# One-column products for the first group's sums of squares, and a fixed order for row 0 of the opening loop

## The chip, the cores and the metric

The kernel runs on one core of a Trainium2 chip. The metric is the device time of one execution in microseconds (us). A core has five engines with a queue of instructions each: TensorE (PE, its weight loads are listed as PEld), VectorE (DVE), ScalarE (ACT), GpSimd (POOL) and SyncE (SP), which here only issues transfers. All wait for one another through semaphores.

## The reference

One layer of a hybrid mixer over 2048 tokens of 1024 columns, with 256 context tokens beside them. What matters here is its beginning:

```python
def rms_norm(x):
    return x * lax.rsqrt(jnp.mean(x * x, axis=-1, keepdims=True) + EPS)

shift, scale, gate = jnp.split(jax.nn.silu(c) @ w_ada[l] + b_ada[l], 3, axis=-1)
h = rms_norm(x) * (1.0 + scale[:, None, :]) + shift[:, None, :]
rq, rk, rv, rg, aq, ak, av, ag = project(h, w_in[l])      # h @ w_in, 13 chunks of 256 columns
```

Behind it stand retention, windowed attention, the output projection, the gated residual and a last norm.

## The kernel before

Tokens are taken in four groups of 512, group 3 first. A group is held transposed: 8 tiles of 128 model columns by 512 tokens, the "rows" k = 0 to 7 of the opening loop. Each operand of a projection is split into a high part, rounded to fp32r, and a low part, the remainder; a projection is three products for each row: high by high, high by low, low by high.

Opening, lines 905 to 952. The row `c` is loaded, spread to all partitions by a product with ones (L205) and put through SiLU on ACT (L206). Group 3 is loaded in four transfers of two rows (`x3`). For each of the four ACT squares one row (L926), DVE the other (L927) and adds them (L928), and PE adds over partitions with a product of 512 columns (L929), so that every partition holds the sums of all 512 tokens. Four DVE instructions then take the diagonal of each 128x128 block (L934), DVE forms the mean (L181), POOL raises it to the power -0.5 (L184), DVE lays the roots out on four diagonals (L189), and PE spreads these to all partitions by products with ones (`spread`, L196). Twelve dummy products on a tile of ones (`warm`, L915) stand in three places.

The opening loop (L972 to 1000) runs over k. `ada` loads two tiles of 128x1024 of the conditioning matrix (`wss`), and DVE multiplies each by the SiLU row and sums it up (`weigh`, L215); with the bias added (L226) this is the shift and scale of 128 columns. At each even k four transfers bring two rows of four chunks of `w_in`; ACT rounds the high parts (L111), DVE and, for chunk `rg1`, POOL take the low parts (L970). `modulate` scales the row (DVE, L231), ACT adds the shift and rounds (`h3h`, L232), and DVE takes the remainder (`h3l`, L233). PE then runs 24 products for the row (L993) into eight banks. Behind the loop come the roots of the next group (L997, from sums of squares that ACT takes of rows of `x`, L176), the weights of chunk `aq0` (L111 and L329), the gates, whose ACT instructions (L591) free banks, and the products of `aq0` (L341).

The program is written in one sequence; a scheduler orders the instructions of each engine by a model of costs and due times, except where `tc.keep_in_program_order` pins an instruction behind all that was written before it on its engine, or `tc.issue_after` (in `behind`) puts those of a block behind a named one on its engine. These order the issue only; each engine runs its queue strictly in order.

Of the kernel before, what the change touches and what calls it, by code (L numbers as in the profile page):

```python
# [16 lines left out]
P = 128  # L17
# [22 lines left out]
def tile_hymba(  # L40
# [111 lines left out]
    class Stats:  # L152
# [24 lines left out]

        def roots(self, on_dve=False):
            r = rsm.tile([P, 2, 4], F32, tag="rs", name=f"r_{self.name}")
            if on_dve:  # L180
                PE["mean"] = dve.tensor_scalar(r[:, 1, : self.nt], self.ss, 1.0 / D, EPS, op0=ALU.mult, op1=ALU.add)  # L181
            else:
                act.activation(r[:, 1, : self.nt], self.ss, AF.Identity, bias=eps1, scale=1.0 / D)
            pool.tensor_tensor(r[:, 0, : self.nt], r[:, 1, : self.nt], half4[:, : self.nt], op=ALU.pow)  # L184
            self.dg = tmp(f"dg_{self.name}")[:, : self.n]
            for t in range(self.nt):
                dst, rt = self.dg[:, t * P : (t + 1) * P], r[:, 0, t : t + 1]
                if on_dve:
                    PE["diag"] = dve.tensor_scalar(dst, ident, rt, None, op0=ALU.mult)  # L189
                else:  # L190
                    act.activation(dst, ident, AF.Copy, scale=rt)

# [7 lines left out]
    def silu_row(t, i):  # L200
        nc.sync.dma_start(t[0:1], crow[i : i + 1])
        for n in range(2):
            s = slice(n * GT, (n + 1) * GT)
            ps = ptp.tile([P, GT], F32, tag="tp", name=f"pc{i}{n}")
            pe.matmul(ps, ones[0:1], t[0:1, s], start=True, stop=True)  # L205
            act.activation(t[:, s], ps, AF.Silu)  # L206
        return t

    def weigh(w, row, a, idle=False):

        if idle:
            pool.tensor_tensor(w, w, row, op=ALU.mult)
            act.activation(w, w, AF.Copy, accum_out=a)
        else:
            dve.scalar_tensor_tensor(w, w, 1.0, row, op0=ALU.mult, op1=ALU.mult, accum_out=a)  # L215

# [3 lines left out]
    def ada(pl, tag, row, kc, which, after=(None, None)):  # L220
        for j in range(2):
            w = pl.tile([P, D], F32, tag=tag, name=f"wss{which}_{kc}_{j}")
            nc.sync.dma_start(w, wss[kc][:, j, :])
            with behind(after[j]):
                weigh(w, row, acc2[:, kc, which, j : j + 1], which and j)
        dve.tensor_tensor(mod[:, kc, which], acc2[:, kc, which], nbada[:, kc:16:8], op=ALU.add)  # L226

    def modulate(x, r, which, ht, k):

        shk, sck = mod[:, k, which, 0:1], mod[:, k, which, 1:2]  # L230
        PE["scaled"] = dve.scalar_tensor_tensor(x, x, sck, r, op0=ALU.mult, op1=ALU.mult)  # L231
        act.activation(ht[0][:, k, :], x, AF.Identity, bias=shk)  # L232
        return dve.scalar_tensor_tensor(ht[1][:, k, :], x, shk, ht[0][:, k, :], op0=ALU.add, op1=ALU.subtract)  # L233
# [682 lines left out]

    row0 = silu_row(st0.tile([P, D], F32, tag="row", name="row0", bufs=1), 0)
# [5 lines left out]
    pss = ptp.tile([P, GT], F32, tag="tp", name="ss_x3")  # L923
# [28 lines left out]

    def start_weights(q):

        for pair in range(2):
            raw = ld.tile([P, 2, 2, 256], F32, tag="ld", name=f"wr_s{pair}_{q}")
            for i in range(2):
                n = CH[2 * pair + i]
                nc.sync.dma_start(raw[:, i], win[CHUNKS.index(n)][:, 2 * q : 2 * q + 2, :])
            for i in range(2):  # L960
                n = CH[2 * pair + i]
                rounded(startw[n][:, 0, 2 * q : 2 * q + 2, :], raw[:, i], "act")
                raws[n] = raw[:, i]

    raws = {}
# [6 lines left out]
    for k in range(NK):  # L972
        ada(st0, "ada", row0, k, 0, (PE["scaled"],) * 2 if k else (PE["mean"], PE["diag"]))
        if k % 2 == 0:
            start_weights(k // 2)
            with behind(None if k else PE["diag"]):
                start_low(k // 2, CH if k else CH[:1])
        modulate(x3[:, k], r3 if k else ps3, 0, H[3], k)
        if k == 0:
            with behind(PE["scaled"]):  # L980
                start_low(0, CH[1:])
            r3 = rp.tile([P, GT], F32, tag="rope", name="r3")
            act.activation(r3, ps3, AF.Copy)
        if k == NK - 2:
# [421 lines left out]
```

## Time and profile before

| | us |
|---|---|
| three timed runs | 1178.88, 1181.79, 1182.34 (median 1181.79) |
| the profiled execution | 1177.99 |
| its span, first to last instruction | 1175.4 |
| PE busy | 1133.2 (96%) |
| DVE busy | 798.2 (68%) |
| ACT busy | 465.7 (40%) |
| POOL busy | 404.5 (34%) |

The profile is of one execution, and its own time is 2.6 us above its span. All moments below are microseconds from the start of the span. Matmuls are pipelined, so a record's length is longer than the step from one to the next. A granted clock of 1.00 is the higher of TensorE's two levels (2.4 GHz), 0.50 the lower (1.2 GHz).

### The profile page before, as it was taken

What the parts mean: (1) busy time and instruction counts of PE and PEld (TensorE: products, weight loads), DVE (VectorE), ACT (ScalarE), POOL (GpSimd) and SP (SyncE); (2) the same over time, 40 slices, a digit from 0 to 9 for tenths busy, and PEclk for the clock granted to TensorE, in tenths of its full rate; (3) what the DMA queues carried; (4) which work ended last, traced back from release to release, by engine and by line L of the source; (5) the groups of instructions that cost most, each with busy time, mean ns of one, the idle gap of its engine ahead of it and who ended that gap; (6) DMA issues with size and microseconds to landing.
All of it is one profiled execution on the core that took longest, in us unless ns stands there. A gap on an engine that the chain in (4) does not pass through costs nothing.

```text
span 1175.4 us, 18111 instructions
## 1 busy us (share of the span) xinstructions
PE 1133.2 (96%) x6290; PEld 973.1 (83%) x6290; DVE 798.2 (68%) x1883; ACT 465.7 (40%) x1025; POOL 404.5 (34%) x517
## 2 busy tenths in 40 slices
PE   7999978999999999999999988999999999999997
PEld 3887857999988889998888877888888888888885
DVE  6974876544783645657666447777777777777774
ACT  3344423432342002331001336555555555555562
POOL 1102654100221200002224335555555555555542
PEclk9998989999999999999999999999999999999999
DMA  8948678542564542533356385444444444444310
GB/s 305 324 152 259 235 228 308 177 132 86 176 215 157 162 125 77 175 119 117 97 162 201 83 210 187 131 130 131 130 130 131 131 130 131 130 130 131 95 37 36
DMA packets 139537, 182.24 MB, mean 155 GB/s; under 512 B 11315, under 2 KB 103091, under 8 KB 139318
## 3 DMA queue, kind: packets, MB, share of 16 engines
q1 hardware_dynamic: 126630, 174.54, 47.3%
q10 hardware_dynamic: 12816, 6.56, 1.8%
q8 instruction: 49, 0.80, 0.3%
q14 instruction: 42, 0.34, 0.1%
HBM read 130.19 MB, written 50.86 MB: 154 GB/s over the span
## 4 chain that ended last, share of the span: by engine, by line
PE 69%; DVE 19%; POOL 3%; ACT 3%; DMA 3%; issue 2%; SPq 1%; DVEq 0%; POOLq 0%; ACTq 0%
PE pz L1205 10%; PE rv L354 8%; PE rk L341 7%; PE aq L341 6%; PE ag L341 6%; PE o L1168 4%; PE rg L341 4%; PE rq L341 4%; PE pt L1155 3%; DVE p L749 3%; DVE phl L1158 3%; PE S L743 3%; PE u L470 2%; PE ak L341 2%; PE S L747 2%
## 5 line engine op out<-in xcount | busy, mean ns | idle before, releaser
L1157 ACT ACTIVATE phl<-pt 128x512 fp32r<-128x512 f32 x156 | 92.7, 595 | 98.8 <-PE pt L1155 96.0
L765 POOL TENSOR_SCALAR p<-p,m 128x640 f32<-128x640 f32 (+1 forms) x128 | 104.1, 814 | 69.9 <-DVE m L764 68.5
L1158 DVE TENSOR_TENSOR phl<-pt,phl 128x512 fp32r<-128x512 f32 x156 | 106.8, 686 | 29.9 <-ACT phl L1157 29.2
L756 ACT ACTIVATE p<-p,m 128x641 f32<-128x641 f32 (+1 forms) x128 | 104.5, 816 | 47.3 <-DVE m L753 47.0
L749 DVE CUSTOM_DVE_ANT_0 p<-S,msk 128x640 f32<-128x640 f32 (+1 forms) x128 | 102.5, 801 | 23.4 <-PE S L747 22.0
L1205 PE MATMUL pz<-wg1h,ma 128*128 128x512 f32 x256 | 106.0, 419 | 0.1
L1205 PE MATMUL pz<-wg0h,mr 128*128 128x512 f32 x256 | 104.0, 409 | 0.6 <-POOL mr L1194 0.4
L1155 PE MATMUL pt<-ident,p 128*128 128x128 f32 x624 | 94.0, 273 | 0.0
L743 PE MATMUL S<-kwin,aq 128*128 128x384 f32 (+1 forms) x256 | 79.2, 332 | 4.2 <-DVE m L749 2.8
L1155 PEld LDWEIGHTS pt<-ident,p 128*128 128x128 f32 x624 | 75.8, 141 | 8.7 <-issue 0.4
L446 ACT ACTIVATE vw<-v,wdec 128x128 fp32r<-128x128 f32 x128 | 43.5, 393 | 80.1 <-DVE v L459 80.1
L747 PE MATMUL S<-kctx,aq 128*128 128x256 f32 x256 | 71.1, 280 | 0.0
L1168 PE MATMUL o<-phl,vwin 128*128 128x512 f32 x184 | 63.1, 422 | 0.8 <-DVE phl L1158 0.6
L743 PEld LDWEIGHTS S<-kwin,aq 128*128 128x128 f32 x256 | 48.0, 188 | 10.7 <-DVE m L749 3.4
L1205 PEld LDWEIGHTS pz<-wg0h,mr 128*128 128x128 f32 x256 | 48.1, 188 | 9.3 <-POOL mr L1194 0.8
L1205 PEld LDWEIGHTS pz<-wg1h,ma 128*128 128x128 f32 x256 | 48.1, 188 | 7.9 <-POOL ma L1183 0.5
L747 PEld LDWEIGHTS S<-kctx,aq 128*128 128x128 f32 x256 | 48.2, 188 | 5.3
L1168 PE MATMUL o<-phl,vctx 128*128 128x512 f32 x128 | 44.7, 414 | 6.8 <-DVE phl L1158 6.7
L1205 PE MATMUL pz<-wg0l,mr 128*128 128x512 f32 x128 | 50.5, 395 | 0.0
L1205 PE MATMUL pz<-wg1l,ma 128*128 128x512 f32 x128 | 50.3, 393 | 0.0
L448 DVE SCALAR_TENSOR_TENSOR vw<-v,wdec,vw 128x128 fp32r<-128x128 f32 x128 | 39.9, 358 | 6.2 <-ACT vw L446 6.2
L780 POOL TENSOR_TENSOR qd<-qkv,decq 128x512 f32<-128x512 f32 x30 | 42.3, 1428 | 1.1
(430 smaller groups left out, 3067.7 us busy)
## 6 DMA issues: line engine op xcount, KB each, us to landing
wss<-in_wss SPq DMA_DIRECT2D x32, 512.0 KB, 6.3
qkv<-d_qkv SPq DMA_DIRECT2D x15, 768.0 KB, 6.2
aq<-d_aq SPq DMA_DIRECT2D x64, 128.0 KB, 3.9
xb<-in_xn SPq DMA_DIRECT2D x16, 512.0 KB, 4.2
out<-xb SPq DMA_DIRECT2D x31, 256.0 KB, 2.3
st<-d_st SPq DMA_DIRECT2D x15, 512.0 KB, 3.8
x<-in_xt SPq DMA_DIRECT2D x12, 512.0 KB, 5.3
xr_x<-in_xn SPq DMA_DIRECT2D x12, 512.0 KB, 3.8
```

Source lines behind the costliest of these rows:

```text
L341: pe.matmul(ps, w[:, a, k, c0 : c0 + P], ht[b][:, k, :], start=(k == 0 and i == 0), stop=(k == NK - 1 and i == 2),)
L354: pe.matmul(ps, ht[a][:, k, t * P : (t + 1) * P], w[:, b, k, :], start=(k == 0 and i == 0), stop=(k == NK - 1 and i == 2),)
L743: i = pe.matmul(psc[:, o:512].rearrange("p (s t) -> p s t", t=P), AQ[b][:, h, :], C2["kwin"][:, kv, hl, ksel], start=(hl == 0), stop=(hl = ...
L747: pe.matmul(psc[:, 512:768], AQ[b][:, h, :], C2["kctx"][:, kv, hl], start=(hl == 0), stop=(hl == 1))
L749: dve.tensor_tensor_reduce(out=pb[:, j, 0:n], in0=psc[:, o : o + n], in1=mk, op0=ALU.add, op1=ALU.max, scale=1.0, scalar=-3e38, accum_out= ...
L756: act.activation(pb[:, j, 0 : n + 1], pb[:, j, 0 : n + 1], AF.Exp, bias=m4[:, 1, j : j + 1], scale=0.125, accum_out=m4[:, 2, j : j + 1],)
L765: pool.tensor_scalar(pb[:, j, 0:n], pb[:, j, 0:n], m4[:, 2, j : j + 1], 0.0, op0=ALU.mult, op1=ALU.add)
L1155: pe.transpose(ppt[:, j], pb[:, j, kt * P : (kt + 1) * P], ident)
L1157: PE["phl"] = act.activation(phl[:, 0], ppt, AF.Copy)
L1158: dve.tensor_tensor(phl[:, 1], ppt, phl[:, 0], op=ALU.subtract)
L1168: pe.matmul(PO[kv], vt, PH[kt][:, hl], start=(kt == 0 and hl == 0), stop=(kt == nkt - 1 and hl == 1))
L1205: pe.matmul(PZ[n2], m[:, a, k % RH, :], WG[k // 4][c][:, k % 4, s], start=(k == 0 and i == 0), stop=(k == NK - 1 and i == 2),)
```

## The change

- The sums of squares of group 3 go to one PSUM tile of 128x4: for each of five parts (the first three pairs added up as before, the two squares of the last pair each by itself) four products with 128 tokens as weights and one column of ones, 20 in all, behind one product with zeros that starts the sums. The diagonals on DVE (L934) go.
- The two halves of the SiLU row's spreading are pinned behind the products of parts 0 and 1.
- Dummy products: 12 at the start, 8 behind the sums, 7 behind the spreading, in place of three times 4.
- Mean and diagonals of the roots are taken on ACT, as for the other groups.
- For k = 0 the first `weigh` is put behind the last square, and the second behind a copy on DVE that reads the roots (`ticked`). ACT rounds one chunk (`rg0`) behind the diagonals and the other three, and the copy `r3`, behind `h3h`; DVE takes the low parts behind the scaling.

```diff
+    warm(12)
     s3 = Stats(GT, "x3")
+    s3.ss = ptp.tile([P, 4], F32, tag="tp", name="ss_x3")
+    tc.keep_in_program_order(pe.matmul(s3.ss, ones, zero4, start=True, stop=False))
     for i in range(4):
         act.activation(sq[0], x3[:, 2 * i], AF.Square)
-        dve.tensor_tensor(sq[1], x3[:, 2 * i + 1], x3[:, 2 * i + 1], op=ALU.mult)
-        dve.tensor_tensor(sq[0], sq[0], sq[1], op=ALU.add)
-        pe.matmul(pss, ones, sq[0], start=(i == 0), stop=(i == 3))
+        PE["square"] = dve.tensor_tensor(sq[1], x3[:, 2 * i + 1], x3[:, 2 * i + 1], op=ALU.mult)
+        if i < 3:
+            dve.tensor_tensor(sq[0], sq[0], sq[1], op=ALU.add)
+        for q in sq[: 1 if i < 3 else 2]:
+            for t in range(4):
+                tc.keep_in_program_order(
+                    pe.matmul(s3.ss[:, t : t + 1], q[:, t * P : (t + 1) * P], ones[:, 0:1], start=False, stop=(part == 4 and t == 3))
+                )
+            part += 1
+        if i < 2:
+            half_row(row0, 0, i)
-    for t in range(4):
-        dve.scalar_tensor_tensor(
-            own[:, ts], pss[:, ts], 1.0, ident, op0=ALU.mult, op1=ALU.mult, accum_out=s3.ss[:, t : t + 1]
-        )
-    warm(4)
-    s3.roots(True)
-    warm(4)
+    warm(8)
+    s3.roots()
+    def ticked(i):
+        with behind(i):
+            return dve.tensor_copy(tick, s3.r[:, 0, 0:1])
     ps3 = s3.spread()
-    warm(4)
+    warm(7)
...
-        ada(st0, "ada", row0, k, 0, (PE["scaled"],) * 2 if k else (PE["mean"], PE["diag"]))
+        ada(st0, "ada", row0, k, 0, (PE["scaled"],) * 2 if k else (PE["square"], ticked))
         if k % 2 == 0:
-            start_weights(k // 2)
+            start_load(k // 2)
             with behind(None if k else PE["diag"]):
-                start_low(k // 2, CH if k else CH[:1])
+                start_high(k // 2, CH if k else CH[:1])
+            if k:
+                start_low(k // 2, CH)
         modulate(x3[:, k], r3 if k else ps3, 0, H[3], k)
         if k == 0:
+            r3 = rp.tile([P, GT], F32, tag="rope", name="r3")
+            with behind(PE["high"]):
+                start_high(0, CH[1:])
+                act.activation(r3, ps3, AF.Copy)
             with behind(PE["scaled"]):
-                start_low(0, CH[1:])
-            r3 = rp.tile([P, GT], F32, tag="rope", name="r3")
-            act.activation(r3, ps3, AF.Copy)
+                start_low(0, CH)
```

## Rows read from the trace of the kernel before

**Rows 1.** The table by stretch: from and to, length, then for PE, PEld, DVE, ACT and POOL the busy time and the number of instructions, then the granted clock, the share of the DMA engines and GB/s.

```profile
25.00:26.00 1.00, 1.00 (x4) 0.81 (x3) 0.96 (x3) 0.00 (x0) 0.00 (x0) 0.50 0.36 66
27.00:28.00 1.00, 1.00 (x6) 0.83 (x5) 1.00 (x1) 0.99 (x2) 0.00 (x0) 1.00 0.94 332
40.00:50.00 10.00, 10.00 (x46) 8.29 (x45) 9.93 (x18) 3.01 (x6) 1.78 (x1) 1.00 0.93 313
60.00:70.00 10.00, 9.30 (x42) 7.38 (x41) 3.85 (x6) 8.30 (x19) 1.02 (x1) 1.00 0.64 228
```

**Rows 2.** The timeline of the opening: start, length, engine, line, operation, tiles, count, and in brackets the idle time before it and what ended it.

```profile
9.50 0.63 ACT L926 ACTIVATE sq_x<-h2x 128x512 f32<-128x512 f32 x1 [0.71 <-DMA h2x<-in_xt]
9.78 0.68 DVE L927 TENSOR_TENSOR sq_x<-h2x 128x512 f32<-128x512 f32 x1
6.38 0.69 DVE L928 TENSOR_TENSOR sq_x<-sq_x,sq_x 128x512 f32<-128x512 f32 x1
7.13 6.75 PE L929 MATMUL ss_x<-sq_x,ones 128*128 128x512 f32 x8 [0.51 <-DVE sq_x L928]
13.99 0.29 DVE L934 SCALAR_TENSOR_TENSOR own_x<-ss_x,ident 128x128 f32<-128x128 f32 x1 [2.73 <-PE ss_x L929]
15.04 1.23 DVE L215 SCALAR_TENSOR_TENSOR wss<-wss,row 128x1024 f32<-128x1024 f32 x1
15.21 1.94 POOL L184 TENSOR_TENSOR r_x<-r_x,half 128x4 f32<-128x4 f32 x1 [13.92 <-DVE r_x L181]
17.14 1.26 POOL L970 TENSOR_TENSOR wrg<-wr_s,wrg 128x512 fp32r<-128x512 f32 x1
17.19 1.87 DVE L189 TENSOR_SCALAR dg_x<-ident,r_x 128x128 f32<-128x128 f32 x4 [0.92 <-POOL r_x L184]
18.62 1.13 PE L196 MATMUL rr_x<-dg_x,ones 128*128 128x128 f32 x8 [3.02 <-DVE dg_x L189]
21.01 0.75 DVE L231 SCALAR_TENSOR_TENSOR h2x<-h2x,mod,rr_x 128x512 f32<-128x512 f32 x1
21.67 1.29 DVE L970 TENSOR_TENSOR w_srq<-wr_s,w_srq 128x512 fp32r<-128x512 f32 x2
21.79 0.72 ACT L232 ACTIVATE h3h<-h2x,mod 128x512 fp32r<-128x512 f32 x1 [5.62 <-DVE h2x L231]
22.56 0.73 PE L993 MATMUL frg<-h3h,wrg 128*128 128x512 f32 x2 [1.95 <-ACT h3h L232]
23.54 1.22 DVE L215 SCALAR_TENSOR_TENSOR wss<-wss,row 128x1024 f32<-128x1024 f32 x1
26.22 0.75 DVE L231 SCALAR_TENSOR_TENSOR h2x<-h2x,mod,r 128x512 f32<-128x512 f32 x1
```

**Rows 3.** The timeline of the end of the loop, and first the scaling of row 5 in its middle.

```profile
47.28 0.75 DVE L231 SCALAR_TENSOR_TENSOR h2x<-h2x,mod,r 128x512 f32<-128x512 f32 x1
59.47 0.72 ACT L232 ACTIVATE h3h<-h2x,mod 128x512 fp32r<-128x512 f32 x1 [1.65 <-DVE h2x L231]
63.35 0.30 ACT L183 ACTIVATE r_x<-ss_x,eps 128x4 f32<-128x4 f32 x1
63.72 1.02 POOL L184 TENSOR_TENSOR r_x<-r_x,half 128x4 f32<-128x4 f32 x1 [10.99 <-ACT r_x L183]
64.77 1.28 ACT L191 ACTIVATE dg_x<-ident,r_x 128x128 f32<-128x128 f32 x4 [1.13 <-POOL r_x L184]
65.96 2.18 ACT L111 ACTIVATE w_s<-wr_s 128x512 fp32r<-128x512 f32 x4
68.67 0.50 PE L341 MATMUL aq<-h3h,w_s 128*128 128x512 f32 x1 [0.70 <-ACT g L591]
```

**Rows 4.** One-column and one-row products elsewhere in the kernel, and the clock beside them: the timeline of PE, then the table by stretch.

```profile
103.20 0.60 PE L168 MATMUL ss_xc<-ones,sqc 128*128 128x1 f32 x4 [0.90 <-DVE sqc L165]
172.98 1.98 PE L205 MATMUL pc<-room,ones 1*128 1x512 f32 x4
2.87 3.75 PE L205 MATMUL pc<-row,ones 1*128 1x512 f32 x4 [2.87 <-DVE nbada L82]
105.00:106.00 1.00, 1.00 (x3) 0.21 (x2) 0.00 (x0) 0.92 (x2) 0.00 (x0) 0.73 0.88 315
106.00:107.00 1.00, 1.00 (x3) 0.10 (x1) 0.00 (x0) 0.06 (x1) 0.00 (x0) 0.50 1.04 380
```

**Rows 5.** A low part on POOL beside DVE, in row 2 of the loop, and the same sum on DVE one row later.

```profile
29.90 1.78 POOL L970 TENSOR_TENSOR wrg<-wr_s,wrg 128x512 fp32r<-128x512 f32 x1 [11.51 <-ACT wrg L111]
30.45 1.26 DVE L226 TENSOR_TENSOR mod<-acc,nbada 128x2 f32<-128x2 f32 x1
36.56 0.16 DVE L226 TENSOR_TENSOR mod<-acc,nbada 128x2 f32<-128x2 f32 x1
```

**Rows 6.** Neighbouring weight loads of the loop's products at the two levels of the clock, and a late wait of PE.

```profile
25.33 0.33 PEld L993 LDWEIGHTS frg<-h3h,wrg 128*128 128x128 f32 x1
25.76 0.33 PEld L993 LDWEIGHTS frq<-h3l,w_srq 128*128 128x128 f32 x1
27.92 0.19 PEld L993 LDWEIGHTS frq<-h3h,w_srq 128*128 128x128 f32 x1
28.15 0.19 PEld L993 LDWEIGHTS frg<-h3h,wrg 128*128 128x128 f32 x1
163.41 1.22 PE L341 MATMUL rq<-h2h,w_brq 128*128 128x512 f32 x2 [6.61 <-DVE w_brq L329]
```

More of the change, by code (lines that the diff above doesn't have):

```diff
@@ L176, in by_row, with roots @@
                 act.activation(x, x, AF.Square, accum_out=self.ss[:, t : t + 1])
[L178 to L183, printed above, removed]
+        def roots(self):
+            r = self.r = rsm.tile([P, 2, 4], F32, tag="rs", name=f"r_{self.name}")
+            act.activation(r[:, 1, : self.nt], self.ss, AF.Identity, bias=eps1, scale=1.0 / D)
             pool.tensor_tensor(r[:, 0, : self.nt], r[:, 1, : self.nt], half4[:, : self.nt], op=ALU.pow)
@@ L202, in silu_row, with half_row @@
         for n in range(2):
[L203 to L207, printed above, removed]
+            half_row(t, i, n)
+    def half_row(t, i, n):
+        s = slice(n * GT, (n + 1) * GT)
+        ps = ptp.tile([P, GT], F32, tag="tp", name=f"pc{i}{n}")
+        tc.keep_in_program_order(pe.matmul(ps, ones[0:1], t[0:1, s], start=True, stop=True))
+        act.activation(t[:, s], ps, AF.Silu)
     def weigh(w, row, a, idle=False):
@@ L214, in weigh @@
         else:
-            dve.scalar_tensor_tensor(w, w, 1.0, row, op0=ALU.mult, op1=ALU.mult, accum_out=a)
+            return dve.scalar_tensor_tensor(w, w, 1.0, row, op0=ALU.mult, op1=ALU.mult, accum_out=a)
     def behind(i):
@@ L223, in ada @@
             nc.sync.dma_start(w, wss[kc][:, j, :])
-            with behind(after[j]):
-                weigh(w, row, acc2[:, kc, which, j : j + 1], which and j)
+            with behind(after[j](i) if callable(after[j]) else after[j]):
+                i = weigh(w, row, acc2[:, kc, which, j : j + 1], which and j)
         dve.tensor_tensor(mod[:, kc, which], acc2[:, kc, which], nbada[:, kc:16:8], op=ALU.add)
@@ L915, in warm @@
             tc.keep_in_program_order(pe.matmul(pd, wones[:, :P], wones, start=True, stop=True))
-    row0 = silu_row(st0.tile([P, D], F32, tag="row", name="row0", bufs=1), 0)
+    row0 = st0.tile([P, D], F32, tag="row", name="row0", bufs=1)
+    nc.sync.dma_start(row0[0:1], crow[0:1])
     x3 = half("h2x3", [P, NK, GT], F32)
@@ L920, in tile_hymba @@
         nc.sync.dma_start(x3[:, 2 * i : 2 * i + 2], xt[3][:, 2 * i : 2 * i + 2])
+    warm(12)
     s3 = Stats(GT, "x3")
-    pss = ptp.tile([P, GT], F32, tag="tp", name="ss_x3")
+    zero4 = rsm.tile([P, 4], F32, tag="zero", name="zero4", bufs=1)
+    dve.memset(zero4, 0.0)
+    s3.ss = ptp.tile([P, 4], F32, tag="tp", name="ss_x3")
+    tc.keep_in_program_order(pe.matmul(s3.ss, ones, zero4, start=True, stop=False))
+    part = 0
     for i in range(4):
@@ L959, in start_weights, with start_high @@
                 nc.sync.dma_start(raw[:, i], win[CHUNKS.index(n)][:, 2 * q : 2 * q + 2, :])
-            for i in range(2):
-                n = CH[2 * pair + i]
-                rounded(startw[n][:, 0, 2 * q : 2 * q + 2, :], raw[:, i], "act")
                 raws[n] = raw[:, i]
+    def start_high(q, chunks):
+        for n in chunks:
+            rounded(startw[n][:, 0, 2 * q : 2 * q + 2, :], raws[n], "act")
     raws = {}
```

13 lines of the change are left out of this document (4 added, 9 removed).

## The prediction, on record before the changed kernel ran

> **What bounds the kernel now.** I read the page first: PE is busy for 96% of the span, DVE for 68%, so only stretches in which PE starves or runs slowly have anything to give. The table by stretch shows where the opening has such places [rows 1]: the clock stands at 0.50 from 25 to 26 and is back at 1.00 from 27 to 28, and PE is short of 0.70 us between 60 and 70. The timeline shows the rest [rows 2]: before its first real product at 22.56 PE has only feeding work (sums 7.13 to 13.88, a wait of 3.02 ahead of the spreading at 18.62, a wait of 1.95 ahead of 22.56). The stretch at the lower level comes about a microsecond after these two waits. Its price: neighbouring weight loads, and with them products, are 0.43 us apart there (25.33 to 25.76) and 0.23 after it (27.92 to 28.15) [rows 6]; eight products at 0.43 in place of 0.23 make some 1.7 us.
>
> From 22.56 on PE is full, but DVE is nearly as full: 9.93 us of the ten from 40 to 50 [rows 1]. Its scalings of row 1 and row 5 stand at 26.22 and 47.28 [rows 2, 3], 5.27 us for a row, where PE needs 24 x 0.227 = 5.44. At the end of the loop a queue on ACT decides when PE goes on: `h3h` of row 7 at 59.47, the squares of the next group, mean, root and diagonals 63.35 to 66.05, the `aq0` roundings to 68.14, then the first gate, behind which PE starts `aq0` at 68.67 after its wait of 0.70 [rows 3]. So what the change is worth is not when PE starts row 0, but how far the chain DVE, ACT and with it 68.67 moves.
>
> **The change part by part.** The sum is made against the profiled execution's own 1177.99 us (span 1175.4 and 2.6 around it). That is 3.8 below the median of the three runs, 1181.79; I carry the difference to the median.
>
> *Squares.* The last transfer is there at 9.50, and the last square ends at 9.78 + 0.68 = 10.46 in both kernels [rows 2]. The fourth addition (0.69) falls away.
>
> *Sums.* Four records of one column take 0.60 in all [rows 4]. Records overlap, so their step is under 0.15; the spreading's eight, of 128 columns, took 1.13 [rows 2], 0.14 with the same tail, and I take 0.12. An f32 product has two records, as the eight for four products in L929 show [rows 2], so four products cost 8 x 0.12 = 0.96, and five parts 4.8. The two halves of the row cost 4 records at 1.98 / 4 = 0.5 at the higher level, 3.75 / 4 = 0.94 at the lower [rows 4]; I take 0.48 to 0.5, so 1.9. The first part can start at the end of the first addition, 7.07 [rows 2]. PE is then busy to 7.12 + 4.8 + 1.9 = 13.8, and with the tail 13.9: the sums end where they ended before. At 0.15 a step they end 1.2 later, and at the lower level, later still, stands a rival. 12 leading dummies at 0.43 each from about 1.6 (the tile of ones is set by then) end near 6.7, ahead of the first part.
>
> *Own sums, mean, root, diagonals.* Before, 13.99 to the scaling at 21.01: 7.0 us. After, identity to root on ACT and POOL takes 1.40 (63.35 to 64.75) [rows 3], so 13.94 to 15.34; four diagonals on ACT 1.28 [rows 3], to 16.64; the spreading ends 0.69 after the last diagonal, as 19.06 to 19.75 [rows 2], so 17.3. On DVE the copy and the held-back second `weigh` (1.23) with its read and `mod` end near 17.0. The scaling comes at 17.35 instead of 21.01, 3.7 earlier, and PE's first product at 18.9. Gone are the diagonals of L934 (0.94), the root's 1.94 in place of 1.02, and the 1.87 of DVE diagonals in place of 1.28, and one `weigh` moves ahead of the root. Eight dummies at 0.22 (1.7) fit between the sums and the first diagonal, seven (1.5) between the spreading and `h3h` (0.75 + 0.72): at the higher level they cost nothing; at the lower they stand in the way, see the first rival.
>
> *Row 0 on DVE.* Before, the next `weigh` starts 2.53 after the scaling (23.54) [rows 2]. After: scaling 0.75, low part of `rg0` in the shade of `h3h` (0.69 beside 0.72), `h3l` 0.7, two low parts 1.3: 3.5. The gain falls by 1.0 to 2.7.
>
> *The part on POOL.* Before, POOL's low part of `rg1` (17.14, 1.26) lay beside the first diagonal, and that was 1.0 longer than the others, a loss that goes. Now it comes after `h3h` and three roundings, some 2.4 us after `h3h`'s start, into DVE's `weigh` and `mod` of row 1. What that costs is seen in row 2: POOL 1.78 instead of 1.26, and the `mod` beside it 1.26 instead of 0.16 [rows 5]. So between nothing, if the two miss each other, and 1.1; I take 1.1, since row 2 is the same pair of instructions. The gain is 1.6.
>
> The Trainium skill ("SBUF — State Buffer", "Who interferes with whom") has a rule for this: a DVE instruction with two inputs in SBUF and a GpSimd one that reads SBUF exclude each other for the whole instruction, and whichever comes first holds the other up. The trace agrees: the root took 1.94 beside a `weigh` and 1.02 alone. The rule speaks for holding the `weigh` behind the root, and against moving the low part: by it the sum is 1.6, without it 2.7.
>
> *Queues.* SP's transfers keep their order; the low parts held back free their raw buffers up to 2 us later after the scaling; as the next such transfers go into others of the seven, I cost that at nothing (0 to 0.5). ACT now has 1.9 us of roundings before `r3`, needed by DVE 5 us later: hidden.
>
> *PE.* It would finish 192 products by 18.9 + 43.5 = 62.4 and starve in small pieces while DVE feeds it; the slow stretch goes, but 1.7 us saved ahead of a wait bring nothing. The first product of `aq0` moves with ACT's queue: 68.67 to 67.1. Behind it PE is full again, so the rest moves along.
>
> Sum: -1.6. 1177.99 becomes 1176.4, and against the median **1180.2**; 1180 it is.
>
> **The rivals.**
>
> *The clock falls among the small products (slower).* Against the forecast speaks the other place with such products: after four one-column records at 103.20 and one-row products at 104.3 the clock went from 1.00 to 0.73 in 105 to 106, and to 0.50 [rows 4]. The opening's own one-row products (0.94 each) ran at the lower level's pace too. For the forecast: the changed opening has more dummies, and 20 products may count otherwise than 2. If it falls near 10, three parts and one row half run at twice the step: the sums end at 17.6; the eight dummies, now 3.4, stand ahead of the spreading on PE's queue, to 21.0; spreading (1.1, or 1.9 at the lower level) to 22.1 or 22.9, scaling 1.1 to 1.9 late. With the 1.0 and 1.1 of row 0 this is +3.2 to +4.0: 1185.4. If the clock never rises before the sums, they end at 20.5, the spreading at 25.8, the scaling 4.9 late, +7.0 in all: 1188.8. The point from which it decides is a granted clock under 1 before about 11.
>
> *Nothing left.* POOL's part catches DVE twice, or the transfers, whose engines are at 0.93 of their time from 40 to 50 [rows 1], can't be moved forward by as much as DVE asks: 0, so 1181.8.
>
> *All of it.* DVE keeps up, since it is 0.17 us a row ahead of PE, the part on POOL misses it, and PE's early start (3.7) and its lost slow stretch (1.7) both count: -5.4, so 1176.4. Against it speaks the wait at 68.67, which ACT ends and not PE.
>
> *Another order further on.* The scheduler's times shift at the front, and later instructions may be issued in another order. The wait of 6.61 at 163.41 for a low part on DVE [rows 6] shows what an order can cost: up to 6.6 less (1175.2) or as much more (1188.4). The trace of before can't show it.
>
> **How the numbers follow.** Forecast 0.42, clock 0.25, nothing left 0.10, all of it 0.13, another order 0.10. 0.3% is 3.5 us, about what a measurement of this kernel can tell from no change. Faster by more: all of it (0.13), half of another order (0.05), and 0.05 of the forecast, as the three runs lie 3.5 apart; 0.23. Slower by more: 0.15 of the clock's 0.25 and half of another order; 0.20. Between: 0.57. The likeliest case's own range is 1178.5 to 1181.8. The range, 1175 to 1187, takes in all of it and the clock falling halfway, and leaves out the clock that never rises and the far ends of another order.
>
> **What would show it.** In the changed profile: the sums end near 13.9, root near 15.3 and alone on POOL with about 1.0, the scaling near 17.35 and `h3h`'s first product near 18.9, with the weight loads of the one-column products at 0.19 and not 0.33; POOL's first low part of `rg1` near 20.5 with a DVE instruction about 1.1 too long beside it; row 1 scaled 1.6 us earlier than 26.22; small waits of PE in the loop; no stretch at 0.50 before 60; `aq` starting near 67.1. The prediction is wrong if the clock is at 0.50 while the sums run, if `aq` starts before 65 or after 69, or if PE's waits between 100 and 170 change by more than 2 us.

## The result and the profile after

The changed kernel took 1184.39 us in the median of 9 runs (1183.4 to 1187.03), the kernel before, beside it, 1179.0 (9 runs, 1177.5 to 1182.34). The ratio is 1.004 with an interval of 1.0026 to 1.0053: slower, by some 5 us. The forecast was 1180: a gain of 1.6, too small to measure, on the 1181.79 that three runs had given for the kernel before.

The page of the changed kernel, from its profiled execution (1183.40 us; before 1177.99):

```profile
span 1181.6 us, 18202 instructions
PE 1143.7 (97%) x6339; PEld 982.0 (83%) x6339; DVE 795.7 (67%) x1871; ACT 466.5 (39%) x1030; POOL 405.2 (34%) x517
```

PE is busier by 10.5 us (1133.2 before). The 15 dummies more would be 3.3 of it at the higher level's pace (15 x 0.22), but all dummies together take 10.35 now (5.26 + 3.42 + 1.67) and took 2.92 before (1.89 + 1.03): most of them run more slowly. DVE has 2.5 us less to do. The timeline of PE in the opening shows where the slow work stands (columns as in [rows 2]):

```profile
1.60 5.26 PE L911 MATMUL warm<-wones 128*128 128x512 bf16 x12 [1.60 <-DVE zero L921]
...
7.05 1.05 PE L935 MATMUL ss_x<-ones,sq_x 128*128 128x1 f32 x8
8.04 1.12 PE L202 MATMUL pc<-row,ones 1*128 1x512 f32 x2
9.09 1.05 PE L935 MATMUL ss_x<-ones,sq_x 128*128 128x1 f32 x8
10.07 2.07 PE L202 MATMUL pc<-row,ones 1*128 1x512 f32 x2
12.07 5.28 PE L935 MATMUL ss_x<-ones,sq_x 128*128 128x1 f32 x24
17.21 3.42 PE L911 MATMUL warm<-wones 128*128 128x512 bf16 x8
20.47 1.05 PE L190 MATMUL rr_x<-dg_x,ones 128*128 128x128 f32 x8
```

The table by stretch has the granted clock beside it (third column from the end):

```profile
10.00:12.00 2.00, 2.00 (x4) 0.55 (x3) 1.29 (x2) 0.31 (x1) 0.00 (x0) 0.53 0.99 373
12.00:14.00 2.00, 2.00 (x10) 1.93 (x10) 1.19 (x2) 1.12 (x2) 0.00 (x0) 0.50 1.00 369
...
18.00:20.00 2.00, 2.00 (x6) 0.76 (x5) 1.20 (x2) 1.20 (x5) 0.77 (x1) 0.50 1.02 407
20.00:22.00 2.00, 2.00 (x13) 1.46 (x12) 0.70 (x4) 0.60 (x2) 0.00 (x0) 0.91 1.05 383
...
24.00:26.00 2.00, 2.00 (x10) 1.65 (x9) 2.00 (x3) 1.11 (x3) 1.29 (x1) 1.00 0.07 20
```

Read them together. Parts 0 and 1 take 1.05 each for 8 records, and the first half of the row 1.12: the higher level. Near 10.1 the clock falls to 0.50 with PE fully busy; the second half takes 2.07, the last three parts 5.28 for 24 records (0.22 a record against 0.13), the eight dummies 3.42. At 20.3 it is back, and the spreading takes 1.05. The sums end at 17.35 instead of 13.88 [rows 2].

The kernel before has slow sums too. Ahead of the first change of the clock that a trace records (6.7 here, 13.3 before) the table prints 1.00 whatever the level is, and only the pace tells it: before, eight records of 512 columns took 6.75, 0.84 each [rows 2], where *cols512* below has two in 1.12. So the change doesn't trade a high clock for a low one: it has the higher level from 6.7 on, and loses it at 10.1 with more than half of its sums to do.

ACT adds a thing of its own, from its timeline:

```profile
9.19 0.60 ACT L203 ACTIVATE row<-pc 128x512 f32<-128x512 f32 x1 [1.77 <-PE pc L202]
9.69 0.62 ACT L928 ACTIVATE sq_x<-h2x 128x512 f32<-128x512 f32 x1
12.18 0.60 ACT L203 ACTIVATE row<-pc 128x512 f32<-128x512 f32 x1 [1.87 <-PE pc L202]
12.67 0.62 ACT L928 ACTIVATE sq_x<-h2x 128x512 f32<-128x512 f32 x1
17.39 0.26 ACT L180 ACTIVATE r_x<-ss_x,eps 128x4 f32<-128x4 f32 x1 [4.10 <-PE ss_x L935]
```

The squares of pairs 2 and 3 (L928) are queued behind the SiLUs of the row's halves (L203), and these wait for PE. So ACT's last square is at 12.67, when its data has long been there (before: 9.50). ACT's squares now wait for products of PE, and PE's last sums need these squares; in this trace PE runs its 24 records in one piece all the same, so the new order costs it nothing here.

Then row 0, from the timelines of DVE, POOL and PE:

```profile
21.56 0.75 DVE L227 SCALAR_TENSOR_TENSOR h2x<-h2x,mod,rr_x 128x512 f32<-128x512 f32 x1 [1.26 <-PE rr_x L190]
...
24.71 1.50 POOL L980 TENSOR_TENSOR wrg<-wr_s,wrg 128x512 fp32r<-128x512 f32 x1 [5.93 <-ACT wrg L111]
24.97 2.31 DVE L211 SCALAR_TENSOR_TENSOR wss<-wss,row 128x1024 f32<-128x1024 f32 x1
...
27.22 1.21 DVE L211 SCALAR_TENSOR_TENSOR wss<-wss,row 128x1024 f32<-128x1024 f32 x1
...
28.75 0.75 DVE L227 SCALAR_TENSOR_TENSOR h2x<-h2x,mod,r 128x512 f32<-128x512 f32 x1
...
71.20 0.50 PE L337 MATMUL aq<-h3h,w_s 128*128 128x512 f32 x1 [0.87 <-ACT g L587]
```

Row 0 is scaled only 0.55 later than before (21.56 against 21.01), row 1 2.53 later (28.75 against 26.22), and `aq0` starts 2.53 later (71.20 against 68.67). The 2.0 between the two rows is DVE's: 3.41 from the scaling to the next `weigh` where it was 2.53, and that `weigh` takes 2.31 beside POOL's low part, and 1.21 alone. Nothing of it is made up again in the loop, in which DVE is full (9.93 us of the ten from 30 to 40, and again from 40 to 50). The DMA engines fall idle meanwhile (0.07 of their time from 24 to 26, 0.48 before): SP's next `wss` wait for buffers that DVE has yet to read.

At `aq0` 2.5 of the 6.2 us between the two spans are there. The rest comes further on; the last experiment shows how much of that is a matter of the execution.

### The profile page after: what moved, and what is told of

It reads as the page before. It is cut to its first block, busy times and chain, and to the rows that moved or that the text cites. A ratio compares the mean times of both kernels' runs of the same rounds, so it can differ in the third digit from the quotient of the medians.

```text
span 1181.6 us, 18202 instructions
## 1 busy us (share of the span) xinstructions
PE 1143.7 (97%) x6339; PEld 982.0 (83%) x6339; DVE 795.7 (67%) x1871; ACT 466.5 (39%) x1030; POOL 405.2 (34%) x517
## 4 chain that ended last, share of the span: by engine, by line
PE 53%; DVE 13%; POOL 2%; ACT 2%; issue 1%; SPq 1%; DMA 1%; DVEq 0%; POOLq 0%; ACTq 0%
PE pz L1219 10%; PE ag L337 5%; PE o L1182 4%; PE rv L350 4%; PE rk L337 4%; PE rg L337 4%; PE aq L337 4%; PE rq L337 4%; PE pt L1169 3%; DVE p L745 3%; DVE phl L1172 3%; PE S L739 2%; PE ak L337 2%; PE S L743 2%; DVE st L824 1%; PE av L337 1%
```

## The experiments

Delays and dummies are added work, whose results go nowhere. Theory C: one-column products let the clock fall, and with the order of row 0's work that makes DVE's rows and `aq0` late. Theory L: part of the difference isn't in the opening, but in which later work the clock's falls hit.

### Sums of 128 columns, and of 512

*wide* keeps everything of the change, ACT's order too, but each of the 20 products moves 128 columns of ones instead of one. Weight loads and the number of instructions are the same; the product with zeros that starts the sums moves 512 columns instead of four.

```diff
-    s3.ss = ptp.tile([P, 4], F32, tag="tp", name="ss_x3")
-    tc.keep_in_program_order(pe.matmul(s3.ss, ones, zero4, start=True, stop=False))
+    wide = ptp.tile([P, GT], F32, tag="tp", name="ss_x3")
+    s3.ss = wide[:, 0:GT:P]
+    tc.keep_in_program_order(pe.matmul(wide, ones, zeros, start=True, stop=False))
...
-                    pe.matmul(s3.ss[:, t : t + 1], q[:, t * P : (t + 1) * P], ones[:, 0:1], start=False, stop=(part == 4 and t == 3))
+                    pe.matmul(wide[:, t * P : (t + 1) * P], q[:, t * P : (t + 1) * P], ones, start=False, stop=(part == 4 and t == 3))
```

> The changed kernel with one edit: each of the 20 products moves 128 columns of ones in place of one, into a bank of 512 columns of which four are read. The weight loads, the order on every engine and all else stay. Theory C (the one-column products let the clock fall, and that alone makes the opening late): no stretch at 0.50 between 8 and 20; the sums end at 14 to 14.5 in place of 17.35, the first scaling is at 18.2 to 18.8 in place of 21.56, aq starts at 67.5 to 68.5 in place of 71.20, and the time falls by 2 to 6 us. Theory O (the fixed order of row 0, with the squares behind the SiLU on ACT and the low part on POOL, makes it late whatever the clock): the scaling moves by less than 1 us, aq by less than 1, and the time by less than 1.

*cols512* goes back to the four products of 512 columns, with the fourth addition and the four diagonals on DVE, inside the changed order.

```diff
-    s3.ss = ptp.tile([P, 4], F32, tag="tp", name="ss_x3")
+    pss = ptp.tile([P, GT], F32, tag="tp", name="ss_x3")
...
+        tc.keep_in_program_order(pe.matmul(pss, ones, sq[0], start=(i == 0), stop=(i == 3)))
...
+        dve.scalar_tensor_tensor(
+            own[:, ts], pss[:, ts], 1.0, ident, op0=ALU.mult, op1=ALU.mult, accum_out=s3.ss[:, t : t + 1]
+        )
```

> The changed kernel with the sums of before: four products of 512 columns and the four diagonals on DVE, all dummies and the order of row 0 as changed. Theory C: the clock stays at 1.00 from 7 on, since these products stream; the last product ends near 12.5, the diagonals near 13.6, the scaling is at 17.5 to 18.5, aq at 67 to 68.5, the time 3 to 6 us below the changed kernel and at most 2 above or 3 below the kernel before. Theory O: scaling after 20.5, aq after 70, no more than 1 us below the changed kernel.

*wide*: 1179.69, ratio 1.001 (0.9995 to 1.0025). PE's timeline and the clock by stretch:

```profile
9.26 1.16 PE L937 MATMUL ss_x<-ones,sq_x 128*128 128x128 f32 x8
10.35 1.12 PE L202 MATMUL pc<-row,ones 1*128 1x512 f32 x2
11.40 3.33 PE L937 MATMUL ss_x<-ones,sq_x 128*128 128x128 f32 x24
...
10.00:12.00 2.00, 2.00 (x11) 1.12 (x11) 1.29 (x2) 0.98 (x2) 0.00 (x0) 1.00 1.00 392
12.00:14.00 2.00, 1.88 (x16) 1.69 (x16) 1.23 (x2) 0.62 (x2) 0.00 (x0) 1.00 1.05 399
```

The clock stays at 1.00; the 24 records that took 5.28 take 3.33, although each moves 128 times as many columns. Row 0 is scaled at 18.04 instead of 21.56, `aq0` starts at 67.69 instead of 71.20. The loss goes, and no gain is left in the time.

*cols512*: 1179.63, ratio 0.9997 (0.9985 to 1.001). The time is as expected, the way to it is not. PE's timeline:

```profile
9.14 1.12 PE L927 MATMUL ss_x<-sq_x,ones 128*128 128x512 f32 x2
...
11.35 3.53 PE L927 MATMUL ss_x<-sq_x,ones 128*128 128x512 f32 x4
```

Here too the clock falls, though the products are wide: it stands at 0.50 from 12 to 14 and is back at 1.00 from 15, 3.4 us in all where the changed kernel has 10.2. (PE had waited 1.37 for its first sum at 7.03.) So the sums end at 14.9 and not near 12.5; row 0 is scaled at 19.26 and `aq0` starts at 68.91, both later than expected, but 2.3 earlier than in the changed kernel. That the loss hangs on the width of the sums' products is shown by *wide*, where little else differs. *cols512* agrees in the time, but doesn't show that wide products keep the clock up.

### A delay put into the kernel before

*delay2* and *delay3* put two or three multiplications of 128x1024 on DVE ahead of row 0's `mod` in the kernel before.

```diff
+        late = kc == 0 and which == 0
+        for _ in range(2 if late else 0):
+            tc.keep_in_program_order(dve.scalar_tensor_tensor(w, w, 1.0, row, op0=ALU.mult, op1=ALU.mult))
...
```

> The kernel before with nothing changed but two more multiplications of DVE on a tile that is done with, between the second weigh and the mod of row 0: 2.3 us at the spot where the changed kernel is late. Theory L (of the 6.2 us between the two profiles 2.5 come from the opening, and the rest from the clock falling at other work further on because the work comes at other moments): aq near 71.0, with the clock at 0.50 for longer in sum after 60 than in the kernel before, in part at the places of the changed kernel (near 188 and 727), and +4 to +6.5 us in all. The rival (a late opening costs what it is late, the rest comes from something else in the change): +2.0 to +2.6 in all, and no new stretch at 0.50.

> The same with three multiplications, 3.45 us. Theory L: aq near 72.1; the time doesn't grow in proportion, but by 3.45 and the stretches at 0.50 that are gained or lost, each 3.4 us of it costing 1.7: +1.5 to +8. The rival: +3.2 to +3.7, and 1.15 more than delay2.

*delay2*: 1180.73, ratio 1.0014 (0.9998 to 1.003). Row 0 is scaled only 0.85 later (21.86) although 2.47 of work were added, since in this execution the clock rose sooner and the sums ended 1.5 earlier, at 12.33; `aq0` starts at 69.67, 1.00 later than before. *delay3*: 1188.41, ratio 1.0079 (1.0053 to 1.0105), sums to 13.52, row 0 scaled at 24.32, `aq0` at 72.09. From the one to the other `aq0` moves by 2.4 us and the median by 7.7. Against the 1179.47 beside them the medians lose 1.3 and 8.9, and neither theory had these sizes: theory L had 4 to 6.5 and 1.5 to 8, its rival 2.0 to 2.6 and 3.2 to 3.7.

The pair isn't clean either: in both builds DVE's work after the scaling is ordered otherwise, so that row 1 is scaled 2.82 and 5.28 later than before where `aq0` is 1.00 and 3.42 later. In *delay3*'s trace, 8.5 us longer than that of before, 3.4 are there at `aq0`, 1.2 at 165, 4.5 at 400 and 8.0 at 726; from 724 to 734 its granted clock is 0.66, where the trace of before has 1.00. So the time is not in proportion to the delay, which speaks against the rival and for theory L; how much of the loss the delay itself makes is not shown.

### Row 0's work ahead of the root

*early* has the sums of 128 columns and another order for row 0: its four chunks are loaded ahead of the first `wss`, ACT rounds all four high parts before the mean, and DVE takes all four low parts, the one of POOL too, before it reads the root.

```diff
-            (pool if n == "rg1" else dve).tensor_tensor(w[:, 1, ks, :], raws[n], w[:, 0, ks, :], op=ALU.subtract)
+            PE["low"] = (pool if n == "rg1" and q else dve).tensor_tensor(w[:, 1, ks, :], raws[n], w[:, 0, ks, :], op=ALU.subtract)
...
+    start_load(0)
+    start_high(0, CH)
+    start_low(0, CH)
     warm(8)
-    s3.roots()
+    with behind(PE["rounded"]):
+        s3.roots()
...
-        with behind(i):
+        with behind(i), behind(PE["low"]):
```

> The changed kernel with sums of 128 columns, row 0's four chunks loaded ahead of its first wss, all their high parts on ACT before the mean, and all low parts of row 0 on DVE before the root, so that POOL and DVE share nothing there and DVE has only h3l between the scaling of row 0 and row 1's weigh. Theory C (an opening that keeps the clock up and is earlier for DVE moves aq0 with it): scaling of row 0 at 17.5 to 18.5, row 1 scaled near 22.8 (before 26.22), aq0 near 65.5 to 66.5 (68.67), no stretch at the lower level before 60 unless at a wait ahead of the spreading; the time 2 to 3 below the kernel before, about 1176.5. Rival (the gain ends on the transfers or on ACT's queue at the loop's end): row 1 is early, the rows after it are not, aq0 at 67.5 or later, the time within 1.2 of before. Rival (where the later stretches at the lower level fall decides): aq0 early, and the time still within 1.2 of before or above it, with longer such stretches after 100.

It took 1176.93 (11 runs) against 1178.81, ratio 0.9987 (0.9975 to 0.9999): a little faster than both kernels. DVE's timeline between the two scalings:

```profile
18.60 0.75 DVE L227 SCALAR_TENSOR_TENSOR h2x<-h2x,mod,rr_x 128x512 f32<-128x512 f32 x1 [0.24 <-PE rr_x L190]
19.27 1.22 DVE L211 SCALAR_TENSOR_TENSOR wss<-wss,row 128x1024 f32<-128x1024 f32 x1
...
22.61 0.75 DVE L227 SCALAR_TENSOR_TENSOR h2x<-h2x,mod,r 128x512 f32<-128x512 f32 x1
```

The `weigh` follows the scaling at once, row 1 is scaled 4.0 behind row 0 instead of 7.2, and `aq0` starts at 65.06, 3.6 earlier than before, as theory C had it. Half of this reaches the median, which lies between that theory and the rival on the falls.

### The same order with one-column products

*early_cols* is *early* with the one-column products back (the first diff of *wide* the other way round). With the changed kernel, *wide* and *early* it makes a square of two orders by two widths.

> The run early with the one-column products of the changed kernel in place of the products of 128 columns: the fourth corner of a square of two orders of row 0 (the changed one; all of it ahead of the root) by two widths of the sums (1; 128). Theory C with costs that add: the clock falls near 10 while the sums run, they end near 17 instead of 14.7, scaling of row 0 near 21 to 22 (early 18.60), row 1 scaled 25 to 26 (22.61), aq0 near 68 to 68.7 (65.06), so the clock's fall costs about 3 here as it does in the changed order (71.20 against 67.69, 3.5); time 1179 to 1181, no difference from before. Rival (the order alone does it, and products of one column only look slow): scaling within 1 of early's 18.6, time within 1 of early's.

1182.01, ratio 1.0018 (1.0008 to 1.0028). PE's timeline:

```profile
13.22 5.28 PE L935 MATMUL ss_x<-ones,sq_x 128*128 128x1 f32 x24
...
18.74 3.19 PE L911 MATMUL warm<-wones 128*128 128x512 bf16 x7 [0.24 <-issue]
21.73 1.72 PE L190 MATMUL rr_x<-dg_x,ones 128*128 128x128 f32 x8
```

The clock falls at 9.5; `aq0` starts at 69.95 instead of 65.06. The fall costs 4.9 here and 3.5 in the changed order (71.20 against 67.69), so a constant 3 was a miss. All moments came 1.2 to 1.5 later than the latest expected, and the time lies a microsecond above its range: with row 0's work out of DVE's way the spreading is all that row 0 waits for (2.04 on DVE), and dummies at the lower level stand ahead of it. ACT's order is not quite the same in the two (three squares ahead of the first SiLU in *early*, two here), but PE has no wait here between 7.39 and the end of the sums at 18.50.

### POOL's low part

*wide_dve* is *wide* with row 0's low part of `rg1` on DVE.

```diff
-            (pool if n == "rg1" else dve).tensor_tensor(
+            (pool if n == "rg1" and q else dve).tensor_tensor(
```

> The run wide with one thing changed: row 0's low part of rg1 on DVE instead of POOL. If the two locked each other (POOL 1.50 beside a DVE weigh of 2.32 instead of 1.22), the weigh is 1.22 again and DVE has one more instruction of 0.7 in its place: row 1 scaled 0.3 to 0.5 earlier than wide's 25.24, aq0 67.1 to 67.5 (67.69); time within 1 of wide's. Rival (the weigh was long for another reason, a DMA or DVE's own read): the weigh stays above 2, row 1 scaled at 25.9.

1180.23, ratio 1.0007 (0.9997 to 1.0016). *wide* first, then *wide_dve*, from their timelines:

```profile
21.19 1.50 POOL L982 TENSOR_TENSOR wrg<-wr_s,wrg 128x512 fp32r<-128x512 f32 x1 [5.04 <-ACT wrg L111]
21.45 2.32 DVE L211 SCALAR_TENSOR_TENSOR wss<-wss,row 128x1024 f32<-128x1024 f32 x1
```

```profile
21.45 0.68 DVE L982 TENSOR_TENSOR wrg<-wr_s,wrg 128x512 fp32r<-128x512 f32 x1
22.06 1.22 DVE L211 SCALAR_TENSOR_TENSOR wss<-wss,row 128x1024 f32<-128x1024 f32 x1
...
24.74 0.75 DVE L227 SCALAR_TENSOR_TENSOR h2x<-h2x,mod,r 128x512 f32<-128x512 f32 x1
```

The `weigh` is at 1.22 again, row 1 comes 0.50 earlier for an instruction of 0.68 more on DVE. An instruction given to POOL to relieve DVE of 0.68 cost DVE 1.10. The rule of the Trainium skill that the prediction cites ("SBUF — State Buffer", "Who interferes with whom") agrees with these rows.

### The dummies

*nodum8* is the changed kernel without the eight dummies ahead of the spreading.

```diff
-    warm(8)
     s3.roots()
```

> The changed kernel without the eight dummies between the sums and the spreading. Theory C prices them at the lower level: 3.42 us on PE's queue from 17.21 to 20.63, with the last diagonal at 20.08. Without them the spreading follows the diagonals, near 20.1 to 20.2 at the lower level, lasts 1.7 to 2.1 instead of 1.05, and the scaling comes at 21.5 to 22.0 (21.56): nothing gained, and the seven dummies and the first products run at the lower level (first product slower to start, the rise of the clock after 23). Time within 1 of the changed kernel's. Rival (the dummies are what makes the opening late): scaling at 20.5, row 1 at 27.7, the time 1 to 2 below the changed kernel's.

1183.04, ratio 1.0037 (1.0023 to 1.0052), beside 1183.74 for the changed kernel. The spreading and the clock after it:

```profile
19.52 2.08 PE L190 MATMUL rr_x<-dg_x,ones 128*128 128x128 f32 x8 [1.91 <-ACT dg_x L185]
...
22.00:24.00 2.00, 2.00 (x7) 0.83 (x6) 1.81 (x4) 1.59 (x3) 0.00 (x0) 0.64 0.83 301
```

The spreading starts a microsecond earlier, takes twice as long, and row 0 is scaled at 21.63 (21.56 with the dummies). They cost a microsecond of queue and buy one of clock.

*mixed* puts three dummies behind each of the five parts instead, to see whether wide products among the narrow ones keep the clock up.

```diff
+            warm(3)
             part += 1
```

> The changed kernel with three dummies of 512 columns behind each of the five parts of one-column products: more work for PE, 15 x 0.22 = 3.3 at the higher level. Theory C (the clock falls because little but one-column products runs): the clock is still at 1.00 at 12, parts take 1.05, the sums end at 16.5 to 17.5 in spite of the added work (17.35 without), scaling near 20.6 (21.56) unless DVE's weigh is last, row 1 scaled near 27.8 (28.75), aq0 near 70.2; time 0 to 2 below the changed kernel's. Rival (the clock falls for another reason at that time, or dummies between don't hold it): it falls near 10 again, the 15 dummies take 0.43 each, the sums end at 20 or later, scaling at 24 or later, time 2 to 5 above the changed kernel's.

1193.2, ratio 1.0123 (1.0091 to 1.0155):

```profile
6.81 1.05 PE L935 MATMUL ss_x<-ones,sq_x 128*128 128x1 f32 x8 [0.95 <-DVE sq_x L931]
7.72 1.36 PE L911 MATMUL warm<-wones 128*128 128x512 bf16 x3
...
10.00:28.00 18.00, 17.78 (x55) 10.32 (x55) 3.99 (x8) 4.29 (x10) 1.04 (x1) 0.50 0.76 270
```

The rival came true, and by more than it said: the time is 9 us above the changed kernel's and not 2 to 5. The clock fell at 7.8, when the first of the added dummies had just started (7.72), so this run can't say whether they would have held it. But it also stayed at 0.50 from 10 to 28 with PE busy for 17.78 of 18 us. Dummies between narrow products did not bring it back, and at the lower level each is one more wait.

### The one-column sums alone

*colsonly* puts the one-column sums into the kernel before and leaves its other orders and dummies.

```diff
...
-        pe.matmul(pss, ones, sq[0], start=(i == 0), stop=(i == 3))
+        for q in sq[: 1 if i < 3 else 2]:
+            for t in range(4):
+                tc.keep_in_program_order(
+                    pe.matmul(s3.ss[:, t : t + 1], q[:, t * P : (t + 1) * P], ones[:, 0:1], start=False, stop=(part == 4 and t == 3))
+                )
+            part += 1
```

> The kernel before with its sums alone replaced by the twenty one-column products (the DVE additions of own sums go too, no leading dummies, the order of everything else left). Theory C: no product ahead of the sums is wide, so the granted clock is 0.50 through all of them (before: it rises at 7.13 or so), each record 0.22 apart, the sums end near 16 (before 13.88) although the last square is there at 10.5; mean and root follow, the scaling comes 0.5 to 2 later than 21.01, since 0.9 of own sums is saved; the time 0 to 3 above the kernel before. Rival (one-column products are harmless by themselves and the changed order is what costs): the clock is up by 10, the sums end by 12.5, the scaling at 20 or before, the time at or below the kernel before.

1180.48, ratio 1.0013 (1.0001 to 1.0025). From the timelines of PE, DVE, ACT and POOL:

```profile
7.09 8.69 PE L937 MATMUL ss_x<-ones,sq_x 128*128 128x1 f32 x40
...
21.63 0.68 DVE L973 TENSOR_TENSOR wrg<-wr_s,wrg 128x512 fp32r<-128x512 f32 x1
...
23.28 0.71 ACT L232 ACTIVATE h3h<-h2x,mod 128x512 fp32r<-128x512 f32 x1
23.46 1.28 POOL L973 TENSOR_TENSOR wrg<-wr_s,wrg 128x512 fp32r<-128x512 f32 x1 [6.35 <-ACT wrg L111]
24.02 1.27 DVE L233 SCALAR_TENSOR_TENSOR h3l<-h2x,mod,h3h 128x512 fp32r<-128x512 f32 x1 [0.44 <-ACT h3h L232]
```

The clock doesn't rise before 21.2: all 40 records run at 0.22, to 15.8. That part is as expected, but for the kernel before, whose clock rises at 13.3 and not near 7.13. At the same lower level its sums took 6.75 [rows 2] and these take 8.69, so without the clock's help the twenty small products are dearer than the four wide ones. The scaling is not later (20.97), since the sums on DVE go and the root no longer shares its time with a `weigh` (1.04 instead of 1.94). Row 1 is 1.6 late all the same, for reasons that I had not foreseen. In this build one low part (0.68) comes behind the scaling, where it came ahead of it before; ACT has the copy `r` and two roundings ahead of `h3h`, for which DVE waits 0.44; and `h3l` takes 1.27 beside POOL's low part instead of 0.75. The run is clean on the clock, not on the time.

### Both kernels a second time

> The changed kernel once more, beside these on one chip. Theory C: the opening is that of its first profile within 0.05 us (clock falls at 10.1, sums end near 17.4, row 0 scaled near 21.56, aq0 at 71.2). Theory L (part of the difference is which later work the clock's falls hit): falls after 100 stand at other moments than 109.1, 163.7, 187.6, 706.4 and 726.9 or have other lengths if the phase differs by execution, and the same ones if they follow from the opening alone. Time 1183 to 1186, ratio 1.003 to 1.005.

> The kernel before once more, for a second trace of it: every other trace has a stretch at the lower level that begins between 720 and 735, and only the first trace of before has none; all others are 1.6 later there. Theory L (which later work the falls hit differs by execution): this trace has such a stretch or others at moments that differ from 105.46, 160.07 and 702.79, and a span of 1175 to 1178. Rival (the falls follow from the kernel alone): the same four stretches within 0.3 us, span 1175.4. Opening as in the first trace in both: row 0 scaled at 21.0, aq0 at 68.7.

*after_again*: 1183.74, ratio 1.0045 (1.0028 to 1.0062); row 0 scaled at 21.85, row 1 at 29.04, `aq0` at 71.48, each 0.3 behind the first trace where 0.05 was expected. *before_again*: 1179.43, ratio 1.0009 (0.9998 to 1.002), profiled execution 1180.17, 2.2 above the first, although its row 0 and `aq0` are 0.46 ahead (20.55 and 68.20; the same moments as in the first were expected). Two stretches of the first trace of before, then of the second:

```profile
180.00:190.00 10.00, 7.61 (x63) 7.41 (x63) 9.02 (x12) 2.98 (x9) 3.81 (x4) 1.00 0.86 281
720.00:730.00 10.00, 8.50 (x46) 7.40 (x47) 7.93 (x31) 4.18 (x9) 4.29 (x8) 1.00 0.26 99
```

```profile
180.00:190.00 10.00, 7.61 (x51) 7.40 (x50) 8.34 (x10) 2.56 (x7) 4.36 (x2) 0.83 0.86 274
720.00:730.00 10.00, 8.06 (x33) 6.82 (x34) 6.59 (x24) 3.04 (x6) 3.78 (x7) 0.83 0.23 87
```

The same kernel has a granted clock of 1.00 in both places in one execution and 0.83 in the other. So which later work a fall hits is a matter of the execution, and the first trace of before was a fortunate one. What that is worth can be followed by pairing equal products in order and taking the start in each trace less that in the first trace of before:

```
about       aq0    120    165    190    400    690    726 us
after      +2.53  +0.86  +2.09  +3.64  +3.87  +4.34  +6.08
again      +2.82  +1.05  +2.58  +4.28  +4.55  +5.70  +6.56
before 2   -0.46  -0.47  -1.56   0.00  -0.02  +0.49  +2.05
early      -3.60  -5.36  -4.00  -2.12  -1.89  -0.91  +0.30
wide_dve   -1.48  -2.97  -2.18  -0.41  -0.13  +1.05  +2.26
```

All rows lose 1.5 to 1.9 between 165 and 190: each of these traces has the clock fall there, and the first trace of before has not. *wide* and *early_cols*, which have no fall there either, lose 0.17 and 0.19. The 0.9 to 1.7 lost from 690 to 726 are of the same kind: only the first trace of before has no fall between 703 and 1170. Against the second trace of before the change is 3.0 late at `aq0`, 3.9 at 400, and 4.0 at 726.

And all traces together, by the moment at which `aq0` starts:

```
            row 0   row 1    aq0    ratio to before
early       18.60   22.61   65.06   0.9987 (0.9975 to 0.9999)
wide_dve    18.04   24.74   67.19   1.0007 (0.9997 to 1.0016)
wide        18.04   25.24   67.69   1.001  (0.9995 to 1.0025)
before 2    20.55   25.76   68.20   1.0009 (0.9998 to 1.002)
before      21.01   26.22   68.67   1
cols512     19.26   26.45   68.91   0.9997 (0.9985 to 1.001)
delay2      21.86   29.04   69.67   1.0014 (0.9998 to 1.003)
early_cols  23.48   27.50   69.95   1.0018 (1.0008 to 1.0028)
colsonly    20.97   27.81   70.24   1.0013 (1.0001 to 1.0025)
after       21.56   28.75   71.20   1.004  (1.0026 to 1.0053)
nodum8      21.63   28.82   71.26   1.0037 (1.0023 to 1.0052)
again       21.85   29.04   71.48   1.0045 (1.0028 to 1.0062)
delay3      24.32   31.50   72.09   1.0079 (1.0053 to 1.0105)
mixed       29.30   36.49   78.94   1.0123 (1.0091 to 1.0155)
```

In every line but those of the two delays, whose builds order the loop's DVE work otherwise, `aq0` stands to before as row 1 does, to 0.02; row 0 alone doesn't order the runs (*early_cols* is 1.9 behind the changed kernel there and 1.25 ahead at `aq0`). The ratio follows `aq0`, at about a microsecond for a microsecond between *early* and the changed kernel (0.0053 x 1179 = 6.2 for 6.1), but before, *cols512* and *colsonly* lie 2 to 3 us under that line, *early_cols* and *delay2* 1.3 and 1.5, and *delay3* lies 3.7 over it. That is not settled.

## Why the prediction was wrong

*The step that failed is "Sums"*: 20 one-column products at 0.12 a step, and dummies that "at the higher level" cost nothing. 0.12 was right for the first two parts (1.05 for 8 records, with the tail), and held at most until 10.1. Then it was 0.22, and the sums ended at 17.35, not 13.9. The width of the products changed the level: *wide* against the changed kernel, 67.69 against 71.20 at `aq0`. Of the traces that begin with twelve dummies, the five with one-column sums have the clock at 0.50 from 7.8 to 10.2 on, for 10 us or longer; the three with sums of 128 columns have no fall before 100. The row that spoke for this was in the prediction, four one-column records at 103.20 before a fall [rows 4]. I set against it that the opening had more dummies and that 20 products "may count otherwise than 2", which no row bore out, and gave it 0.25.

*The rival "the clock falls among the small products"* had the mechanism and most of the sizes: sums to 17.6 (17.35), dummies 3.4 (3.42), spreading to 22.1 at the soonest (21.5), scaling 1.1 to 1.9 late (0.55). The scaling was better since the clock came back at 20.3, ahead of the spreading. Its time of 1185.4 stands against 1184.39, and that it comes so close is in part luck: it was 3.6 on a base of 1181.8, and measured are 5.4 on 1179.0. As the mechanism it should have been the forecast, or near it. The base that was 2.8 too high also makes the forecast of 1180 look nearer than it was: -1.6 was forecast, and +5.4 came.

*"Squares"*: the last one was put at 10.46 "in both kernels". It ends at 13.29 on ACT, behind a SiLU that waits for PE. The pinned order of PE makes ACT's order of squares and SiLUs matter, and I followed only DVE and the transfers there. In *wide* this order stands as well and PE is not kept waiting by it (sums from 11.40 in one piece), so it is not what the loss hangs on.

*"Row 0 on DVE"* and *"the part on POOL"* were right: 3.41 from scaling to `weigh` for 3.5, and 2.31 - 1.21 = 1.1 for the lock, the upper end of the bounds, shown by *wide_dve*.

*The own forecast, had the clock stayed up*, is *wide*: root to diagonals 15.11 to 17.46, scaling 18.04 for 17.35 (the parts took 1.1 each with 128 columns, and the sums ended at 14.7), `aq0` at 67.69 for 67.1, so -0.98 for -1.6. And of that nothing is seen in the time (1.001). "The rest moves along" behind `aq0` was wrong in size: from `aq0` to the end the traces lose 1.3 to 3.9 us against the first trace of before (*delay3* 5.1, *wide* 8.8), and the second trace of before loses 2.6 itself.

*"Nothing left"*: the DMA engines did become idle and late, but behind DVE, whose reads free the buffers. *"All of it"* is not what *early* did, though it shows that 3.6 can be had at `aq0` when DVE is relieved, not PE. *"Another order further on"*: the queues of SP and POOL kept their order to the last instruction; this rival is out for the change. It is what happened to *colsonly* and the two delays.

*What stays open*: of the 5 us of the median, 2.5 to 3.3 are there at `aq0`, and up to a further microsecond by 400. Why the rest tends to a loss in the runs, and why *delay3* loses 9 for 3.4, was not tried further.

## What to carry to other kernels

A product that is cheaper by its columns can be dearer by its clock: before wide products become many narrow ones, look up in the trace what the granted clock did after such products elsewhere, and let that row set the forecast until a run contradicts it. In a loop whose DVE is full, ask when the second row starts: what was moved between the first row's scaling and the second's came out at `aq0` one for one here. And where two traces of one kernel differ by 2 us in where the clock falls, a part of a gain of 2 us can't be read from one pair of traces.

## What the runs showed of the hardware that was not expected

- The granted clock fell to 0.50 while PE was busy for 2.00 of 2.00 us, and stayed there through 17.78 busy of 18 us in *mixed*; with the same number of weight loads and 128 columns a product it stayed at 1.00.
- One-column products are not the only work among which it falls: in *cols512* it stood at 0.50 from 12 to 14, with PE busy for all of that time with products of 512 columns.
- Eight dummies at the lower level cost about what they brought: with them the clock was back at 20.3 and the spreading took 1.05, without them it was back only after 22 and the spreading took 2.08.
- In *wide*'s profiled execution (1185.02, the slowest of its ten) a transfer was late near the end of the first half, and PE stood for it; from its timeline:

```profile
689.73 2.08 PE L783 MATMUL s<-first 128*128 128x128 f32 x8 [3.92 <-DMA first<-d_qkv]
```

In the first trace of before PE is busy for 10.00 us of 680 to 690. So a single trace can be 6.5 us late at one place (*wide* goes from -1.75 at 680 to +4.79 at 690 against before), and the median of its runs doesn't show it. What held the transfer up is not known; *wide_dve*, with the same sums, goes from -0.51 to +1.05 there.
